# Stick-breaking attention: TensorE's work laid down in groups by a string, the mask as two 64-row products per head, one scan and one product for two heads

## The chip, the cores and the metric

The kernel runs on one core of a Trainium2 chip. The metric is the device time of the program in microseconds: 917.52 before, the median of three runs (916.94 to 918.17).

## What is computed

One decoder layer over 512 tokens of width 1024, in float32: a half-step SwiGLU feed-forward (FFN), then a mixer whose two halves, a gated linear recurrence (RG-LRU) and stick-breaking attention with 8 heads of 64, read one normalised input and end in one output projection, then a second FFN. The part that is changed is the attention:

```python
z = jnp.einsum("bhqd,bhkd->bhqk", qb, kf)
causal = k_pos[None, :] < q_pos[:, None]
log_beta = jax.nn.log_sigmoid(z)
log_1m = jnp.where(causal, jax.nn.log_sigmoid(-z), 0.0)
tail = lax.cumsum(log_1m, axis=log_1m.ndim - 1, reverse=True) - log_1m
w = jnp.where(causal, jnp.exp(log_beta + tail), 0.0)
return jnp.einsum("bhqk,bhkd->bhqd", w, vf)
```

A weight is thus sigmoid(z) at its key times the product of sigmoid(-z) over all later keys before the query. The kernel computes it in that form: two sigmoids, a running product from right to left, one multiplication.

## The kernel before

Matrix products run in float32r, a form that keeps part of the mantissa; each operand is split into a high and a low part (`h`, `l`), and three products (high-high, high-low, low-high) stand for one. `mm3` (line 135) issues the three. ScalarE makes the high part, VectorE the low one.

The program runs FFN a, the mixer and FFN b one after another. Within the mixer come the projections for the recurrence and for q, k and v; `turn("k", nk)` (called from line 757) transposes the normalised k by 128-row blocks into `ptk`, from which ScalarE writes `kTh` and VectorE `kTl` (lines 731, 732). It is called after step 27 of the 32 steps of the v projection; `rnn_out` (products `gel`, then `yrh` and `yrl`) is called after step 13. Then comes the attention stage.

There the queries of a head fall into blocks of 128. A unit is one pair of heads with query block 3 (512 keys), block 2 (384 keys), or blocks 1 and 0 (256 + 128), so there are 12 units in 4 pairs. A unit passes through these steps:

- `weigh` (line 799): the scores `pz`. Each head has 64 rows of q and k, so its product takes half of TensorE's rows; the two heads of a pair take one half each. Then the causal mask is added into PSUM by a bf16 product of 128 rows per head (line 821): the identity times `fut`, which holds -1e30 above the diagonal. ScalarE writes `s` = sigmoid(-z) and `be` = sigmoid(z) (lines 826, 828). VectorE runs one scan per head and query block (line 831), `rest`, and multiplies `be` by it (line 841).
- `turn_weights` (line 844): TensorE transposes `be` into `pw`, and ScalarE copies it to `wt` (line 859).
- `attend` (line 862), once for a pair: v times `wt` into `py`, the two heads in two halves of the columns (tiles of 128 rows by 64 columns).
- `take` splits `py` into `yah` and `yal` and sums squares for the attention norm.

Between them stands `project_out(k, 0, ...)` (line 768): the recurrence's part of one 128-row block of the output projection, 12 products `po`, which VectorE adds to x (line 781). Its weights are split as `h_o`, `l_o`. Behind the stage come the attention's part of the projection (24 products for each two blocks) and FFN b.

Each engine works through its own list in order. The order in the lists comes from a scheduler that simulates a timeline; `tc.issue_after` binds an instruction behind another. Which `weigh` and which `project_out` stand after which `turn_weights` is set by the numbers in WEIGH, FILL and REST. PSUM tiles come from pools (`psum("att", z=4, w=3, y=1)`): four banks in turn for `pz` and `po`, three for `pw`, one for `py`; a tile waits until the last reader of the bank's earlier tile is done.

Of the kernel before, what the change touches and what calls it, by code (L numbers as in the profile page):

```python
# [15 lines left out]
P = 128  # L16
T = 512
# [18 lines left out]

WEIGH = (1, 4, 5, 7, 9, 10, 13, 15, 16, 19)
FILL = (4, 8, 12, 16)
REST = (18, 23, 23)
# [9 lines left out]
def hybrid_layer_kernel(  # L49
# [61 lines left out]
    ident_b = const.tile([P, P], BF16, tag="ident_b", name="ident_b")  # L111
    nc.vector.tensor_copy(ident_b, ident)
    fut_b = const.tile([P, P], BF16, tag="fut_b", name="fut_b")
    nc.vector.tensor_copy(fut_b, fut)
# [20 lines left out]
    def mm3(out_, wh, wl, ah, al, start, stop):  # L135
        nc.tensor.matmul(out_, wh, ah, start=start, stop=False)  # L136
        nc.tensor.matmul(out_, wh, al, start=False, stop=False)  # L137
        nc.tensor.matmul(out_, wl, ah, start=False, stop=stop)  # L138
# [612 lines left out]
    def gate_and_recur():  # L751
# [6 lines left out]
        2, "v", {9: lambda: yn.rsqrt(DR, "b"), 13: rnn_out, 27: lambda: turn("k", nk)}  # L758
# [11 lines left out]
    def project_out(k, c, yh, yl, tag, ws, after=None):  # L770
        wh, wl = ws
        pt = bank(f"po{c}_{k}", tag)
        with tc.issue_after(after.ins) if after else nullcontext():
            for j in range(NJ):
                s = slice(j * P, (j + 1) * P)
                mm3(pt, wh[:, s], wl[:, s], yh[j], yl[j], j == 0, j == NJ - 1)
# [16 lines left out]
    with tc.tile_pool(name="att", bufs=2, reuse_waits="tile") as ap:  # L793
        beta = {}
        yah, yal = [], []
        na = Normed("t")

        def weigh(qbs, pair):
# [3 lines left out]
            parts = []  # L802
            for qb in qbs:
                n = (qb + 1) * P
                nn = max(n, 256)
                parts.append((col, n))
                both = None
                for a, b in (("qh", "kh"), ("qh", "kl"), ("ql", "kh")):
                    with tc.issue_after(both.ins) if both else nullcontext():
                        for pz, h in zip(pzs, pair):  # L810
                            j, rows = h // 2, slice((h % 2) * HD, (h % 2 + 1) * HD)
                            both = nc.tensor.matmul(
                                pz[:, col : col + nn],
                                qkT[a][rows, j, qb * P : (qb + 1) * P],
                                qkT[b][rows, j, :nn],
                                start=a + b == "qhkh",
                                stop=False,
                            )
# [4 lines left out]
            for pz, h in zip(pzs, pair):  # L823
                u = f"{qbs[0]}_{h}"
                s = ap.tile([P, T], F32, tag="s", name=f"s{u}")
                nc.scalar.activation(s[:, :col], pz[:, :col], AF.Sigmoid, scale=-1.0)
                be = ap.tile([P, T], F32, tag="be", name=f"be{u}", bufs=5)
                nc.scalar.activation(be[:, :col], pz[:, :col], AF.Sigmoid)
# [197 lines left out]
```

## Time and profile before

| What | Value |
|---|---|
| median of three runs | 917.52 us |
| profiled execution | 917.45 us, its span 915.7 us |
| TensorE busy (PE) | 909.1 us, 99% |
| VectorE busy (DVE) | 668.7 us, 73% |
| ScalarE busy (ACT) | 443.7 us, 48% |
| GpSimd busy (POOL) | 77.0 us, 8% |
| chain that ended last | PE 98%, DVE 1%, ACT 0% |

The span runs from the first to the last instruction of the profiled execution. An engine's share says in how much of it an instruction was under way; TensorE's instructions overlap, so a stretch can count as busy and still hold gaps in which no column is fed. The chain follows the work that ended last backwards. In the rows, L812 is line 812; PE is TensorE, DVE VectorE, ACT ScalarE, POOL GpSimd; a tile such as 64*128 is rows by columns of TensorE's array, and the PEclk of a window is the mean granted clock as a share of 2.4 GHz.

### The profile page before, as it was taken

The numbers are of one execution on the slowest core, as the hardware profiler recorded it, in microseconds if no ns is written. First come the engines' busy times: TensorE is split into PE (matmuls) and PEld (weight loads), VectorE is DVE, ScalarE is ACT, GpSimd is POOL, SyncE is SP. The second block draws the span as 40 slices with busy tenths as digits, with TensorE's granted clock in tenths as the row PEclk, the third lists the DMA queues.
The fourth block names the chain that finished last, engine by engine and source line by source line (L and its number), as shares of the span: only waits on it lengthen the run. The fifth ranks groups of instructions, "written<-read, shape, count | busy, mean of one in ns | idle before, by whom it ended". The sixth has DMA issues, their size and how long they took to land.

```text
span 915.7 us, 13632 instructions
## 1 busy us (share of the span) xinstructions
PE 909.1 (99%) x5410; PEld 798.7 (87%) x5410; DVE 668.7 (73%) x1031; ACT 443.7 (48%) x745; POOL 77.0 (8%) x57
## 2 busy tenths in 40 slices
PE   9999999999999999999999999999999999999998
PEld 8888899889988998888876678888899989998997
DVE  7599788658865859855689858399679756884663
ACT  7343456335533546445666744443356424642450
POOL 0000000000000005644030010500000000000000
PEclk9999999999999999999999999999999999999999
DMA  8532123502351123322111123522222422242102
GB/s 270 200 124 58 46 102 129 161 26 93 109 170 62 48 92 113 111 98 71 47 57 37 47 93 119 203 75 70 70 92 93 161 69 93 93 161 87 47 25 92
DMA packets 27807, 89.51 MB, mean 98 GB/s; under 512 B 3040, under 2 KB 6368, under 8 KB 23648
## 3 DMA queue, kind: packets, MB, share of 16 engines
q1 hardware_dynamic: 27744, 88.65, 28.7%
q8 instruction: 42, 0.69, 0.3%
q14 instruction: 21, 0.17, 0.1%
HBM read 86.54 MB, written 2.10 MB: 97 GB/s over the span
## 4 chain that ended last, share of the span: by engine, by line
PE 98%; DVE 1%; ACT 0%; issue 0%
PE pxgb L371 5%; PE pxga L371 5%; PE pxub L371 5%; PE pxua L371 5%; PE pdb L136 4%; PE pdb L138 4%; PE pdb L137 4%; PE pda L136 4%; PE pda L138 4%; PE pda L137 4%; PE pygb L371 4%; PE pyga L371 4%; PE pyua L371 4%; PE pyub L371 4%; PE first_p L501 4%; PE po L136 2%
## 5 line engine op out<-in xcount | busy, mean ns | idle before, releaser
L137 PE MATMUL pdb<-hlb,h_db 128*128 128x512 f32 (+1 forms) x180 | 68.7, 385 | 0.0
L138 PE MATMUL pdb<-hhb,l_db 128*128 128x512 f32 (+1 forms) x180 | 68.7, 385 | 0.0
L137 PE MATMUL pda<-hla,h_da 128*128 128x512 f32 x176 | 68.0, 389 | 0.0
L138 PE MATMUL pda<-hha,l_da 128*128 128x512 f32 x176 | 67.9, 389 | 0.0
L136 PE MATMUL pdb<-hhb,h_db 128*128 128x512 f32 (+1 forms) x180 | 67.3, 385 | 0.0
L136 PE MATMUL pda<-hha,h_da 128*128 128x512 f32 x176 | 66.2, 389 | 0.0
L441 DVE SCALAR_TENSOR_TENSOR x<-pdb,x 128x512 f32<-128x512 f32 (+1 forms) x33 | 21.9, 673 | 49.0 <-PE pdb L138 49.0
L441 DVE SCALAR_TENSOR_TENSOR x<-pda,x 128x512 f32<-128x512 f32 x32 | 21.8, 688 | 39.9 <-PE pda L138 39.9
L126 ACT CAST h_da<-r_da 128x768 fp32r<-128x768 f32 (+1 forms) x28 | 24.1, 868 | 48.2 <-PE pda L137 21.0
L126 ACT CAST h_db<-r_db 128x768 fp32r<-128x768 f32 (+1 forms) x28 | 24.3, 868 | 45.5 <-PE pdb L137 22.9
L137 PEld LDWEIGHTS pdb<-hlb,h_db 128*128 128x128 f32 x180 | 33.8, 188 | 6.6
L138 PEld LDWEIGHTS pdb<-hhb,l_db 128*128 128x128 f32 x180 | 33.8, 188 | 6.5
L136 PEld LDWEIGHTS pdb<-hhb,h_db 128*128 128x128 f32 x180 | 33.8, 188 | 6.5
L137 PEld LDWEIGHTS pda<-hla,h_da 128*128 128x128 f32 x176 | 33.1, 188 | 6.7
L138 PEld LDWEIGHTS pda<-hha,l_da 128*128 128x128 f32 x176 | 33.1, 188 | 6.7
L136 PEld LDWEIGHTS pda<-hha,h_da 128*128 128x128 f32 x176 | 33.1, 188 | 6.6
L166 POOL TENSOR_TENSOR sqa_m<-sqa_m,sq_m 128x512 f32<-128x512 f32 x7 | 11.8, 1690 | 313.3 <-ACT sq_m L165 313.1
L371 PE MATMUL pxga<-xh_sa,l_ga 128*128 128x256 f32 x128 | 36.2, 283 | 0.0
L371 PE MATMUL pxgb<-xh_sb,l_gb 128*128 128x256 f32 x128 | 36.2, 283 | 0.0
L371 PE MATMUL pxga<-xl_sa,h_ga 128*128 128x256 f32 x128 | 36.2, 283 | 0.0
L371 PE MATMUL pxgb<-xl_sb,h_gb 128*128 128x256 f32 x128 | 36.2, 283 | 0.0
L371 PE MATMUL pxua<-xh_sa,l_ua 128*128 128x256 f32 x128 | 36.2, 283 | 0.0
(397 smaller groups left out, 3105.3 us busy)
## 6 DMA issues: line engine op xcount, KB each, us to landing
r_da<-in_wd SPq DMA_DIRECT2D x24, 384.0 KB, 3.3
r_db<-in_wd SPq DMA_DIRECT2D x24, 384.0 KB, 3.2
rga<-in_wg SPq DMA_DIRECT2D x8, 1024.0 KB, 4.8
rua<-in_wu SPq DMA_DIRECT2D x8, 1024.0 KB, 4.7
rgb<-in_wg SPq DMA_DIRECT2D x8, 1024.0 KB, 5.5
rub<-in_wu SPq DMA_DIRECT2D x8, 1024.0 KB, 4.8
r_gb<-in_wg SPq DMA_DIRECT2D x6, 512.0 KB, 3.1
r_ub<-in_wu SPq DMA_DIRECT2D x6, 512.0 KB, 3.5
```

The costliest lines, as they stand in the source:

```text
L126: nc.scalar.copy(hi, raw)
L136: nc.tensor.matmul(out_, wh, ah, start=start, stop=False)
L137: nc.tensor.matmul(out_, wh, al, start=False, stop=False)
L138: nc.tensor.matmul(out_, wl, ah, start=False, stop=stop)
L166: (engine or nc.gpsimd).tensor_add(self.acc, self.acc, sq)
L371: nc.tensor.matmul(pt, l[:, s], r, start=start and k == 0 and i == 0, stop=k == KD // 2 - 1 and i == 2, skip_group_check=True,)
L441: nc.vector.scalar_tensor_tensor(x[k][:, t], pt[:, t], 0.5, x[k][:, t], op0=ALU.mult, op1=ALU.add)
L501: nc.tensor.matmul(pts[i], wp[i][:, s], xp[k], start=k == 0 and wp is hi and xp is n1.h, stop=k == KD - 1 and wp is lo,)
```

## The change

The three tables of numbers give way to one string, STEPS. Its letters stand for one `weigh` (Z), one `turn_weights` for a whole unit (W), one `project_out` of the recurrence's part (F) and one `attend` with `take` (P); every group of TensorE instructions is bound behind the last instruction of the group before it. The mask's identity and `fut` are stored as two halves of 64 rows, once for each half of the array, and each head adds its mask by two products of 64 rows on its own half. `s`, `be` and `rest` hold two heads side by side, and one scan and one product run over a unit. To start anew at each head and query block, the scan takes the maximum with `marks`, a tensor that is 1 at the starts and 0 elsewhere (the product stays at or below 1), in place of adding zero. `turn("k", ...)` comes after step 22 instead of 27. The buffers of `be` go from 5 to 3 (of twice the size), those of `rest` from 2 to 1.

```diff
-WEIGH = (1, 4, 5, 7, 9, 10, 13, 15, 16, 19)
-FILL = (4, 8, 12, 16)
-REST = (18, 23, 23)
+STEPS = "ZFZFZWZFWZWFZWZPWZFWZWZPWZFWZWPWWFPF"
...
+    halves_b = []
+    for src, n in ((ident, "ident_b"), (fut, "fut_b")):
+        t = const.tile([P, 2, P], BF16, tag=n, name=n)
+        for half in range(2):
+            for to in range(2):
+                nc.vector.tensor_copy(t[to * HD : (to + 1) * HD, half, :], src[half * HD : (half + 1) * HD, :])
...
-        2, "v", {9: lambda: yn.rsqrt(DR, "b"), 13: rnn_out, 27: lambda: turn("k", nk)}
+        2, "v", {9: lambda: yn.rsqrt(DR, "b"), 13: rnn_out, 22: lambda: turn("k", nk)}
...
+        def step():
+
+            return tc.issue_after(last[-1].ins) if last else nullcontext()
...
-                for pz in pzs:
-                    nc.tensor.matmul(pz[:, col + n - P : col + n], ident_b, fut_b, start=False, stop=True)
+                for half in range(2):
+                    with step():
+                        for i in range(2):
+                            rows = slice(i * HD, (i + 1) * HD)
+                            both = nc.tensor.matmul(
+                                pzs[i][:, col + n - P : col + n],
+                                ident_b[rows, half, :],
+                                fut_b[rows, half, :],
+                                start=False,
+                                stop=half == 1,
+                            )
+                    last.append(both)
...
-                for c, n in parts:
-                    nc.vector.tensor_tensor_scan(
-                        rest[:, c : c + n - 1][:, ::-1],
-                        s[:, c + 1 : c + n][:, ::-1],
-                        zero.to_broadcast([P, n - 1]),
-                        1.0,
-                        op0=ALU.mult,
-                        op1=ALU.add,
-                    )
-                for c, n in parts:
-                    w = be[:, c : c + n - 1]
-                    nc.vector.tensor_mul(w, w, rest[:, c : c + n - 1])
+            flat = [t.rearrange("p h c -> p (h c)") for t in (s, be, rest)]
+            n = 2 * col - 1
+            nc.vector.tensor_tensor_scan(
+                flat[2][:, :n][:, ::-1],
+                flat[0][:, 1:][:, ::-1],
+                marks[qbs][:, 1:][:, ::-1],
+                1.0,
+                op0=ALU.mult,
+                op1=ALU.max,
+            )
+            nc.vector.tensor_mul(flat[1][:, :n], flat[1][:, :n], flat[2][:, :n])
...
+        for what in STEPS:
+            if what == "Z":
+                scored.append(weigh(*units[len(scored)]))
+            elif what == "W":
...
+                turn_weights(qbs, scored[turned], ws[pair])
+                turned += 1
+            elif what == "F":
+                w = weights_out(done_f, 0, 1)
+                with step():
+                    project_out(done_f, 0, yrh, yrl, "z", *w)
+                last.append(project_out.last)
+                done_f += 1
+            else:
+                py = bank(f"py{done_p}", "y")
+                attend(pairs[done_p], py, ws[pairs[done_p]])
+                take(done_p, py)
+                done_p += 1
```

Three places in the lists show what moves. First VectorE between the sums of the recurrence's norm (`m_r`) and the first split that follows; `kTl` appears once for each block of 128 tokens. Before:

```order
L181 TENSOR_SCALAR m_r<-pst_r 128x4
L128 TENSOR_TENSOR l_o_2_4889<-r_o_2_4885,h_o_2_4887 128x512
L658 TENSOR_TENSOR gel_3770<-gel_3770,rb_r 128x512
L658 TENSOR_TENSOR gel_3790<-gel_3790,rb_r 128x512
L658 TENSOR_TENSOR gel_4058<-gel_4058,rb_r 128x512
L658 TENSOR_TENSOR gel_4181<-gel_4181,rb_r 128x512
L732 SCALAR_TENSOR_TENSOR kTl<-ptk_4548,vec,kTh 128x4x128
L732 SCALAR_TENSOR_TENSOR kTl<-ptk_4555,vec,kTh 128x4x128
L732 SCALAR_TENSOR_TENSOR kTl<-ptk_4562,vec,kTh 128x4x128
L662 SCALAR_TENSOR_TENSOR yrl_4477<-gel_3770,vec,yrh_4475 128x512
L662 SCALAR_TENSOR_TENSOR yrl_4482<-gel_3790,vec,yrh_4480 128x512
L732 SCALAR_TENSOR_TENSOR kTl<-ptk_4569,vec,kTh 128x4x128
```

Now, from the first `kTl` on:

```order
L734 SCALAR_TENSOR_TENSOR kTl<-ptk_4533,vec,kTh 128x4x128
L734 SCALAR_TENSOR_TENSOR kTl<-ptk_4540,vec,kTh 128x4x128
L734 SCALAR_TENSOR_TENSOR kTl<-ptk_4547,vec,kTh 128x4x128
L130 TENSOR_TENSOR l_o_2_4776<-r_o_2_4772,h_o_2_4774 128x512
L660 TENSOR_TENSOR gel_3776<-gel_3776,rb_r 128x512
L660 TENSOR_TENSOR gel_3796<-gel_3796,rb_r 128x512
L660 TENSOR_TENSOR gel_4064<-gel_4064,rb_r 128x512
L660 TENSOR_TENSOR gel_4187<-gel_4187,rb_r 128x512
L664 SCALAR_TENSOR_TENSOR yrl_4483<-gel_3776,vec,yrh_4481 128x512
L664 SCALAR_TENSOR_TENSOR yrl_4488<-gel_3796,vec,yrh_4486 128x512
L664 SCALAR_TENSOR_TENSOR yrl_4493<-gel_4064,vec,yrh_4491 128x512
L734 SCALAR_TENSOR_TENSOR kTl<-ptk_4554,vec,kTh 128x4x128
```

Three quarters of `kTl` stand ahead of the `gel` products now; the fourth stands behind them and behind three `yrl`.

Second, TensorE at the first `attend` (`py`; the names `wt_` are the two heads' weights). Before:

```order
L812 MATMUL pz_2_4844<-kTh,qTh 128x256
L812 MATMUL pz_3_4845<-kTh,qTh 128x256
L866 MATMUL py_4815<-wt_4675,v_4591 64x512
L849 MATMUL pw_3_4838<-ident,be_3_4760 128x128
L866 MATMUL py_4815<-wt_4676,v_4591 64x512
L866 MATMUL py_4815<-wt_4675,v_4593 64x384
L866 MATMUL py_4815<-wt_4676,v_4593 64x384
L866 MATMUL py_4815<-wt_4675,v_4595 64x256
L866 MATMUL py_4815<-wt_4676,v_4595 64x256
L866 MATMUL py_4815<-wt_4675,v_4597 64x128
L866 MATMUL py_4815<-wt_4676,v_4597 64x128
L849 MATMUL pw_3_4838<-ident,be_3_4760 128x128 x3
```

Now:

```order
L844 LDWEIGHTS ident_b
L844 MATMUL pz_5_4901<-fut_b,ident_b 128x128
L899 MATMUL py_4921<-wt_4737,v_4597 64x512
L899 MATMUL py_4921<-wt_4738,v_4597 64x512
L899 MATMUL py_4921<-wt_4737,v_4599 64x384
L899 MATMUL py_4921<-wt_4738,v_4599 64x384
L899 MATMUL py_4921<-wt_4737,v_4601 64x256
L899 MATMUL py_4921<-wt_4738,v_4601 64x256
L899 MATMUL py_4921<-wt_4737,v_4603 64x128
L899 MATMUL py_4921<-wt_4738,v_4603 64x128
L880 MATMUL pw_0_4936<-ident,be_2_4815 128x128 x3
L880 MATMUL pw_1_4937<-ident,be_2_4815 128x128 x3
```

Before, a transpose of the second head's weights stands inside the group, and the scores of the unit around it are cut too; now each group stands whole.

Third, VectorE from the first scan on. Before:

```order
L831 SCALAR_TENSOR_TENSOR rest_0_4621<-s_0_4617,zero 128x511
L841 TENSOR_TENSOR be_0_4619<-be_0_4619,rest_0_4621 128x511
L831 SCALAR_TENSOR_TENSOR rest_1_4628<-s_1_4624,zero 128x511
L841 TENSOR_TENSOR be_1_4626<-be_1_4626,rest_1_4628 128x511
L831 SCALAR_TENSOR_TENSOR rest_0_4645<-s_0_4641,zero 128x383
L831 SCALAR_TENSOR_TENSOR rest_1_4652<-s_1_4648,zero 128x383
L841 TENSOR_TENSOR be_0_4643<-be_0_4643,rest_0_4645 128x383
L841 TENSOR_TENSOR be_1_4650<-be_1_4650,rest_1_4652 128x383
L781 TENSOR_TENSOR x_91<-po_0_4661,x_91 128x512
```

Now:

```order
L863 SCALAR_TENSOR_TENSOR rest_0_4638<-s_0_4636,marks_4613 128x1023
L871 TENSOR_TENSOR be_0_4637<-be_0_4637,rest_0_4638 128x1023
L783 TENSOR_TENSOR x_97<-po_0_4651,x_97 128x512
L130 TENSOR_TENSOR l_o_4_4971<-r_o_4_4967,h_o_4_4969 128x512
L863 SCALAR_TENSOR_TENSOR rest_0_4679<-s_0_4677,marks_4616 128x767
L871 TENSOR_TENSOR be_0_4678<-be_0_4678,rest_0_4679 128x767
L783 TENSOR_TENSOR x_98<-po_1_4692,x_98 128x512
```

The scans (listed under the name of their instruction class) of two heads are one; the sum of the second output block into x, which frees a bank of `pz`, stands behind the second unit.

## Rows read from the trace of the kernel before

**Rows 1.** Windows of two stretches: time, busy us (instructions) per engine, PEclk, DMA.
```profile
474.00:484.00 10.00, 8.16 (x41) 5.34 (x40) 9.79 (x14) 7.91 (x16) 0.00 (x0) 0.83 0.08 28
474.70:544.70 70.00, 67.65 (x385) 45.60 (x385) 56.52 (x91) 46.53 (x101) 2.86 (x2) 0.98 0.15 53
```

**Rows 2.** TensorE timeline: start, us, engine, line, op, tiles, [idle <-releaser].
```profile
474.67 0.51 PE L812 MATMUL pz<-kTh,qTh 64*128 64x512 f32 x2
477.01 0.51 PE L812 MATMUL pz<-kTl,qTh 64*128 64x512 f32 x2 [1.84 <-DVE kTl L732]
```

**Rows 3.** Waits from 474 to 545: engine, releaser, total us, times, longest.
```profile
DVE rest L831 <- ACT s L826: 1.9, 3, 1.2
PE pw L849 <- DVE be L841: 0.5, 1, 0.5
```

**Rows 4.** VectorE timeline before the first scan.
```profile
470.50 2.50 DVE L658 TENSOR_TENSOR gel<-gel,rb_r 128x512 f32<-128x512 f32 x4 [2.08 <-ACT rb_r L197]
476.21 0.75 DVE L732 SCALAR_TENSOR_TENSOR kTl<-ptk,vec,kTh 128x512 fp32r<-128x512 f32 x1
```

**Rows 5.** TensorE timeline: transposes, score products, mask, transposes.
```profile
502.07 0.49 PE L849 MATMUL pw<-ident,be 128*128 128x128 f32 x3
502.49 0.50 PE L812 MATMUL pz<-kTh,qTh 64*128 64x512 f32 x2
502.83 0.40 PE L812 MATMUL pz<-kTl,qTh 64*128 64x512 f32 x2
503.07 0.39 PE L812 MATMUL pz<-kTh,qTl 64*128 64x512 f32 x2
503.39 0.29 PE L821 MATMUL pz<-fut_b,ident_b 128*128 128x128 bf16 x2
503.51 0.39 PE L849 MATMUL pw<-ident,be 128*128 128x128 f32 x2
```

**Rows 6.** TensorE timeline: attend in two pieces, and in one.
```profile
494.37 1.07 PE L866 MATMUL py<-wt,v 128*64 128x512 f32 x2
495.63 2.37 PE L866 MATMUL py<-wt,v 128*64 128x512 f32 x14
...
509.44 2.37 PE L866 MATMUL py<-wt,v 128*64 128x512 f32 x16
```

**Rows 7.** VectorE timeline: scans, products, sum into x, split.
```profile
504.33 1.22 DVE L831 TENSOR_TENSOR_SCAN rest<-s,zero 128x511 f32<-128x511 f32 x1 [0.56 <-ACT s L826]
505.66 0.69 DVE L841 TENSOR_TENSOR be<-be,rest 128x511 f32<-128x511 f32 x1
508.19 0.95 DVE L831 TENSOR_TENSOR_SCAN rest<-s,zero 128x383 f32<-128x383 f32 x1
509.28 0.56 DVE L841 TENSOR_TENSOR be<-be,rest 128x383 f32<-128x383 f32 x1
510.62 0.67 DVE L781 TENSOR_TENSOR x<-po,x 128x512 f32<-128x512 f32 x1
511.20 0.69 DVE L128 TENSOR_TENSOR l_o<-r_o,h_o 128x512 fp32r<-128x512 f32 x1
```

**Rows 8.** VectorE timeline: a scan over two tensors.
```profile
451.48 2.34 DVE L649 TENSOR_TENSOR_SCAN tau<-dec,ix 128x512 f32<-128x512 f32 x2
```

**Rows 9.** ScalarE timeline: sigmoids of the first score tile.
```profile
477.95 0.60 ACT L826 ACTIVATE s<-pz 128x512 f32<-128x512 f32 x1 [0.47 <-PE pz L821]
478.44 0.59 ACT L828 ACTIVATE be<-pz 128x512 f32<-128x512 f32 x1
```

**Rows 10.** VectorE timeline: the last products with the scans.
```profile
530.82 0.60 DVE L841 TENSOR_TENSOR be<-be,rest 128x255 f32<-128x255 f32 x2
```

**Rows 11.** TensorE timeline: after those products, and the FFN's first product.
```profile
531.71 0.47 PE L136 MATMUL po<-yah,h_o 128*128 128x512 f32 x1
...
564.52 0.39 PE L136 MATMUL pgb<-xh_b,h_gb 128*128 128x512 f32 x1
```

**Rows 12.** VectorE timeline: its first weights.
```profile
4.50 0.29 DVE L483 CAST first_h<-first_r 128x256 fp32r<-128x256 f32 x1 [2.69 <-DMA first_r<-in_wg]
```

More of the change, by code (lines that the diff above doesn't have):

```diff
@@ L793, in hybrid_layer_kernel @@
     with tc.tile_pool(name="att", bufs=2, reuse_waits="tile") as ap:
-        beta = {}
         yah, yal = [], []
         na = Normed("t")
+        marks = {}
+        for qbs in ((3,), (2,), (1, 0)):
+            w = sum(qb + 1 for qb in qbs) * P
+            m = ap.tile([P, 2 * w], F32, tag=f"m{qbs[0]}", name=f"marks{qbs[0]}", bufs=1)
+            nc.gpsimd.memset(m, 0.0)
+            for head in range(2):
+                c = head * w
+                for qb in qbs:
+                    c += (qb + 1) * P
+                    if c < 2 * w:
+                        nc.gpsimd.memset(m[:, c - 1 : c], 1.0)
+            marks[qbs] = m
+        last = []
+        def step():
+            return tc.issue_after(last[-1].ins) if last else nullcontext()
         def weigh(qbs, pair):
@@ new lines, in weigh @@
+                col += n
+            u = f"{qbs[0]}_{pair[0]}"
+            s = ap.tile([P, 2, col], F32, tag="s", name=f"s{u}")
+            be = ap.tile([P, 2, col], F32, tag="be", name=f"be{u}", bufs=3)
+            rest = ap.tile([P, 2, col], F32, tag="rest", name=f"rest{u}", bufs=1)
+            for i in range(2):
+                nc.scalar.activation(s[:, i, :], pzs[i][:, :col], AF.Sigmoid, scale=-1.0)
+            for i in range(2):
+                nc.scalar.activation(be[:, i, :], pzs[i][:, :col], AF.Sigmoid)
@@ new lines, in weigh, with turn_weights @@
+            flat = [t.rearrange("p h c -> p (h c)") for t in (s, be, rest)]
[9 more added lines that the diff above has]
+            nc.vector.tensor_mul(flat[1][:, :n], flat[1][:, :n], flat[2][:, :n])
+            return be
+        def turn_weights(qbs, be, ws):
+            nb = sum(qb + 1 for qb in qbs)
+            pws = [bank(f"pw{qbs[0]}_{i}", "w") for i in range(2)]
+            for i, (pw, wt) in enumerate(zip(pws, ws)):
+                with step():
+                    for b in range(nb):
+                        turned = nc.tensor.transpose(
+                            pw[:, b * P : (b + 1) * P], be[:, i, b * P : (b + 1) * P], ident
+                        )
+                last.append(turned)
+                c = 0
+                for qb in qbs:
+                    n = qb + 1
+                    src = pw[:, c * P : (c + n) * P].rearrange("p (b q) -> p b q", b=n)
+                    first = max(qb - 2, 0) * P
+                    q = slice(qb * P - first, (qb + 1) * P - first)
+                    to = wt[:, first : first + 4 * W].rearrange("p (b q) -> p b q", b=4)[:, :n, q]
+                    nc.scalar.copy(to, src)
+                    c += n
@@ L862, in attend @@
         def attend(pair, py, ws):
             for b in range(NB):
[L865 to L872 removed]
+                with step():
+                    for i, h in enumerate(pair):
+                        both = nc.tensor.matmul(
+                            py[i * HD : (i + 1) * HD, b * P :],
+                            v[b][:, h * HD : (h + 1) * HD],
+                            ws[i][:, b * W + b * P : b * W + T],
+                            start=b == 0,
+                            stop=b == NB - 1,
+                        )
@@ L874, in take @@
+                last.append(both)
         def take(j, py):
```

94 lines of the change are left out of this document (16 added, 78 removed).

## The prediction

> **What bounds the kernel now.** I read the busy time by stage first, then TensorE's timeline across the attention stage, then who waits for whom there, then VectorE's timeline. In the 70 us from the first score product on, TensorE has work in 67.65 us, VectorE in 56.52 and ScalarE in 46.53 [rows 1]: TensorE ends the stage, VectorE stands close behind it. In those records TensorE truly waits only twice, 1.84 us for the last quarter of kTl [rows 2] and 0.5 us for weights that VectorE had not multiplied yet [rows 3]. The rest of its loss lies inside its busy time: the half clock after the first wait, the gaps when it changes between tiles of 64 and 128 rows, and attend products that run alone. So the question is how much of that the new order takes away, and whether VectorE can follow.
>
> **TensorE, term by term.** The wait for kTl. VectorE stands idle 2.08 us before the four gel products [rows 4] and makes all of kTl behind them; the last quarter starts at 476.21 and takes 0.75, so pz resumes at 477.01 [rows 2, 4]. In the new order three quarters of kTl come ahead of gel, in that idle time. The fourth comes behind four gel products and three yrl, which are of its own kind: 470.50 + 2.44 + 3 x 0.67 + 0.75 = 475.7 (each starts 0.08 before the last one ends), or about 475.2 if the copy of rb_r comes half a microsecond sooner because nothing stands before it on TensorE. pz asks for it one pair after 474.67, at 475.0. So 0.2 to 0.7 of the 1.84 us stay; I take 0.3, a gain of 1.5.
>
> The clock. From 474 to 484 the granted clock averages 0.83 [rows 1], that is, some of it ran at 1.2 instead of 2.4 GHz, right after the wait of 1.84 us; 0.17 of 10 us is 1.7 us of work lost. With the wait at 0.3 I count it as gained.
>
> Changes of tile. Three transposes 0.11 apart from 502.07 on should let pz start at 502.40; it starts at 502.49 (+0.09). The first pair of pz products takes 0.34 to the next, the second 0.24 (+0.10), the third, before the mask product of 128 rows, 0.32 (+0.08) [rows 5]. A trip into the 64-row tiles and back costs 0.27. Counted over the two orders, from the first pz to the sums of the attention norm, the tile shape changes 58 times before and 29 times now (the mask keeps the shape, and the groups are no longer cut): 14.5 trips, 3.9 us. The mask itself: 64 products of 64 rows stand for 32 of 128. The old ones took 0.06 each (two from 503.39 to 503.51) [rows 5]. If the two heads' halves run beside each other, as the pz pairs do (both in 0.51 [rows 2]), they take the time of 32; if not, 32 x 0.06 = 1.9 us more, which VectorE's pace, below, would partly cover. I take the first, because it is the same pair of tiles.
>
> Attend. In the order before, one of the two heads' first products stands apart in three of the four pairs: that lone one takes 1.07, and the remaining 14 rows still 2.37, as long as a whole group of 16 elsewhere [rows 6]. A loss of 1.0 each, of which 0.2 are tile changes counted already: 3 x 0.8 = 2.4.
>
> Sum for TensorE alone: 1.5 + 1.7 + 3.9 + 2.4 = 9.5 us.
>
> **VectorE, which must keep up.** Scans: 511 columns 1.22, 383 columns 0.95 [rows 7], so 0.0021 us per column and 0.14 fixed. The new scan reads a real tensor of marks and takes a maximum, where the old one read a broadcast zero and added. The trace has a scan over two real tensors: 512 columns twice in 2.34, at most 1.17 each [rows 8], so I price marks at nothing; the maximum is not in the trace, see the last rival. 1023 columns then take 2.28, 767 take 1.74. The product waits 0.11 for its scan (504.33 + 1.22 to 505.66) and takes 0.69 for 511 and 0.56 for 383 [rows 7], hence 1.22 and 0.95, of which 0.08 overlap the next. One unit: 2.28 + 0.11 + 1.22 - 0.08 = 3.53, or 1.74 + 0.11 + 0.95 - 0.08 = 2.72. All twelve: 4 x 3.53 + 8 x 2.72 = 35.9. Between the first scan and the last product of the new order stand six sums into x, four splits of 512 columns and two yal, at 0.58 to 0.67 [rows 7], and two splits of 1024: 12 x 0.6 + 2 x 1.15 = 9.5. Together 45.4 us without a pause.
>
> The first scan now needs both heads: the mask is done at 475.9, two s and one be come 0.49 apart and the last takes 0.60 [rows 9], so it starts at 475.9 + 0.15 + 0.98 + 0.60 = 477.6. The last product ends at 477.6 + 45.4 + 0.1 = 523.1; before, at 530.82 + 0.60 = 531.4 [rows 10]. From there TensorE before still had the work from 531.71 to the next FFN at 564.52 [rows 11], 32.8 us. Now, behind the last product, it has six transposes (0.7 with their wait) and the same output products, with the attend whole: 0.7 + 32.8 - 1.0 = 32.5. End: 523.1 + 32.5 = 555.6, 8.9 us sooner. That is less than TensorE's 9.5: **VectorE sets the pace now.**
>
> What stops TensorE instead. pz and po share four PSUM banks in turn; the second head of unit 4 gets the bank of po_1, which is free when VectorE has added po_1 to x, behind the product of unit 2. VectorE: 477.6 + 3.53 + 0.58 + 0.6 + 2.72 + 0.67 = 485.7. TensorE is there at 475.9 + 2.9 (po_0) + 0.9 + 2.9 + 1.2 + 0.9 = 484.7. So it waits about 1 us, and likewise, shorter, at units 7 and 10. These waits lie within the 8.9, but the clock may fall after them. I deduct 0.7 for that (two fifths of 1.7) and 0.8 for VectorE waiting for s, which it does for 1.9 us in all before [rows 3]. Forecast: 8.9 - 1.5 = 7.4 gained.
>
> **What costs nothing.** Eight copies of 64 rows instead of two at the start: they run before VectorE's first weights, for which it waits 2.69 us [rows 12]. The fills of the marks are on GpSimd, which does nothing from 474 to 484 [rows 1], and the unit that asks for the last of them is the third. ScalarE does the same activations of the same size.
>
> **Rivals.** (a) TensorE's gain arrives whole: VectorE's 0.8 of waits is not there and the clock stays up, while the kTl wait goes entirely. 9.5 + 0.3 = 9.8 gained, 907.7. For it: VectorE already waits for s in only three places. Against: it has no slack left in the new order.
>
> (b) The clock falls after each of the three new waits. The one case in the trace is a wait of 1.84 us, after which the mean clock is 0.83 [rows 1, 2]; after 0.5 us nothing falls. At 1 us it may go either way. Three times 1.7 us, little of it covered: 8.9 - 5.1 = 3.8 gained, 913.7. The Trainium skill has this in "TensorE: Matmul & The Clock Gate", section "A second HAM failure mode: psum-queue depth-cycling": cycling through PSUM banks can leave so many short idle spots between groups of products that the clock swings between its two levels. By that rule the time would be the one just given; the case before shows it once.
>
> (c) The change does not do what it says: TensorE's gaps in that stage are covered by what it waits for anyway, and the regrouping only moves them. Then the wait and its clock are all that goes, 1.5 + 1.7 = 3.2 gained, 914.3. Against it: TensorE's records show no waits there to cover them [rows 3].
>
> (d) Slower: a scan with a maximum against marks read backwards. It decides over 4 x 1023 + 8 x 767 = 10,228 columns, and VectorE has no slack, so each 0.001 us per column is 10.2 us. From 0.0009 more (0.0021 to 0.0030) the gain is gone; half as much again, 0.00105, gives 10.7 - 8.9 = 1.8 lost, 919.3. For it: no row shows a maximum. Against: the scan with other tensors costs the same [rows 8].
>
> **How the numbers follow.** The profiled execution took 917.45 us, 0.07 under the median of the three runs. Forecast 917.45 - 7.4 = 910.0, chance 0.62; its own range is 908.5 to 912. Rivals: (a) 0.13, (b) 0.11, (c) 0.08, (d) 0.06. The range of 907.2 to 914.0 holds the forecast, (a) and (b) and leaves out most of (c) and (d). About 0.2% either way, 1.8 us, is what a measurement here can tell from no change: faster 0.90, within it 0.04, slower 0.06.
>
> **What would show it.** Right: pz<-kTl waits under 0.7 us and the clock stays at full around 477; VectorE goes from the first scan to the last product with under 2 us of pauses, 46 to 47 us; TensorE waits for x at units 4, 7 and 10; attend is four blocks of 2.37; a scan of 1023 columns takes 2.3. Wrong: a scan above 3 us, mask products in the 64-row tiles apart by more than 0.12, or a granted clock under 0.9 in several stretches.

## The result, and the profile after

912.21 us (median of 4 runs, 910.77 to 912.53) against 917.62 before (4 runs, 916.94 to 918.17): a ratio of 0.9938, interval 0.9921 to 0.9956. That is 5.4 us faster; the forecast was 7.4. The profiled execution took 912.53 us, its span 910.8.

| | before | after |
|---|---|---|
| profiled execution, span | 917.45, 915.7 | 912.53, 910.8 |
| first score product | 474.67 | 475.75 |
| first scan on VectorE | 478.80 | 478.82 |
| end of the last product with the scans | 531.4 | 526.0 |
| first product of FFN b | 564.52 | 559.60 |

From the first product of FFN b to the end both take 351.2 us (915.7 - 564.52 and 910.8 - 559.60), so all of the difference lies in the attention stage. There VectorE starts its first scan at the same time in both kernels and ends its last product with the scans 5.4 us sooner; what TensorE has left behind that is 0.5 longer (33.1 to 33.6). Of VectorE's 52.6 us before, 4.4 were idle: three waits for `s` [rows 3] and three for the high part of the attention's output, which in the view of VectorE's waits from 474 to 530 is this row:

```profile
DVE yal L879 <- ACT yah L877: 2.5, 3, 1.4
```

In the changed kernel none of that idle time is left. First the windows after, which answer to [rows 1]:

```profile
474.00:484.00 10.00, 10.00 (x60) 7.16 (x60) 8.30 (x10) 8.06 (x16) 0.00 (x0) 1.00 0.09 28
475.80:545.80 70.00, 66.89 (x448) 49.41 (x448) 53.39 (x49) 45.38 (x100) 6.54 (x4) 0.98 0.18 63
524.00:534.00 10.00, 7.83 (x31) 6.15 (x33) 4.47 (x5) 3.03 (x8) 1.28 (x1) 0.83 0.15 54
```

At 474 the clock is now at full; the fall that [rows 1] show there stands at 524 instead. TensorE's timeline says what lies around it, the answer to [rows 2, 5 and 11]:

```profile
467.41 0.63 PE L728 MATMUL ptk<-ident,natk 128*128 128x128 f32 x4 [0.62 <-DVE m_r L183]
475.75 0.50 PE L830 MATMUL pz<-kTh,qTh 64*128 64x512 f32 x2
476.09 0.39 PE L830 MATMUL pz<-kTl,qTh 64*128 64x512 f32 x2
487.02 0.49 PE L830 MATMUL pz<-kTh,qTh 64*128 64x512 f32 x1 [0.76 <-DVE x L783]
510.78 2.37 PE L899 MATMUL py<-wt,v 128*64 128x512 f32 x16
526.17 1.51 PE L880 MATMUL pw<-ident,be 128*128 128x128 f32 x6 [2.35 <-DVE be L871]
527.33 0.78 PE L138 MATMUL po<-yrh,h_o 128*128 128x512 f32 x1
559.60 0.39 PE L138 MATMUL pgb<-xh_b,h_gb 128*128 128x512 f32 x1
```

The wait for kTl is gone and each attend is one block of 2.37. In their place stand three waits: 0.62 for a block of the normalised k (the row names m_r, which VectorE finished just then; the transposes read natk), 0.76 for x at unit 4, and 2.35 for VectorE's last product. Behind that one TensorE runs at 1.2 GHz, until about 529.5 (the first po takes 0.78 instead of 0.50).

VectorE from the first scan on, the answer to [rows 7 and 10]:

```profile
478.82 2.29 DVE L863 TENSOR_TENSOR_SCAN rest<-s,marks 128x1023 f32<-128x1023 f32 x1 [1.43 <-ACT s L858]
481.21 1.23 DVE L871 TENSOR_TENSOR be<-be,rest 128x1023 f32<-128x1023 f32 x1
482.35 0.68 DVE L783 TENSOR_TENSOR x<-po,x 128x512 f32<-128x512 f32 x1
...
487.48 1.75 DVE L863 TENSOR_TENSOR_SCAN rest<-s,marks 128x767 f32<-128x767 f32 x1
489.33 0.96 DVE L871 TENSOR_TENSOR be<-be,rest 128x767 f32<-128x767 f32 x1
490.39 2.29 DVE L863 TENSOR_TENSOR_SCAN rest<-s,marks 128x1023 f32<-128x1023 f32 x1
...
519.78 1.75 DVE L871 TENSOR_TENSOR be<-be,rest 128x767 f32<-128x767 f32 x1
...
525.06 0.96 DVE L871 TENSOR_TENSOR be<-be,rest 128x767 f32<-128x767 f32 x1
```

No row between the first scan and the last product has an idle time: VectorE is the pace, for 47.2 us. A scan with marks and a maximum costs what the old one did per column (2.29 for 1023). Two things are slower than they need be. Where a scan follows a product with nothing between, it starts 1.06 behind the product's start; where something stands between, that starts 0.88 behind (485.40 to 486.28): the one buffer of `rest` is still being read. And the product at 519.78 takes 1.75 instead of 0.96, beside this row of GpSimd:

```profile
518.70 2.01 POOL L168 TENSOR_TENSOR sqa_t<-sqa_t,sq_t 128x512 f32<-128x512 f32 x1 [47.80 <-ACT sq_t L167]
```

The product starts in the middle of it and ends 0.82 behind its end, about its own length. The addition itself begins under the scan of 517.91, which keeps its 1.74, and takes 2.01 where the next one takes 1.28 (at 528.26). The Trainium skill ("SBUF — State Buffer", section "Who interferes with whom") says that a VectorE instruction with two inputs in SBUF and a GpSimd instruction that reads SBUF exclude each other; these rows agree.

ScalarE ahead of the first scan, the answer to [rows 9]:

```profile
476.56 0.70 ACT L765 ACTIVATE v<-pv,r_m 128x512 f32<-128x512 f32 x1
477.14 0.61 ACT L858 ACTIVATE s<-pz 128x512 f32<-128x512 f32 x1
477.61 0.62 ACT L860 ACTIVATE be<-pz 128x512 f32<-128x512 f32 x1
478.09 0.63 ACT L858 ACTIVATE s<-pz 128x512 f32<-128x512 f32 x1
```

The scan needs both `s`; between them stands a `be`, and ahead of them the last copy of v.

### The profile page after: what moved, and what is told of

Its sections match the earlier page's. It is cut to its first block, busy times and chain, and to the rows that moved or that the text cites. A ratio compares the mean times of both kernels' runs of the same rounds, so it can differ in the third digit from the quotient of the medians.

```text
span 910.8 us, 13645 instructions
## 1 busy us (share of the span) xinstructions
PE 902.8 (99%) x5442; PEld 797.8 (88%) x5442; DVE 668.1 (73%) x997; ACT 442.9 (49%) x745; POOL 80.5 (9%) x65
## 4 chain that ended last, share of the span: by engine, by line
PE 94%; DVE 3%; ACT 1%; issue 1%; POOL 1%; DVEq 0%; POOLq 0%
PE pxga L373 5%; PE pxgb L373 5%; PE pxub L373 5%; PE pxua L373 5%; PE pdb L140 4%; PE pdb L139 4%; PE pdb L138 4%; PE pda L138 4%; PE pda L139 4%; PE pda L140 4%; PE pygb L373 4%; PE pyga L373 4%; PE pyub L373 4%; PE pyua L373 4%; PE first_p L503 4%; PE po L138 2%
## 5 line engine op out<-in xcount | busy, mean ns | idle before, releaser
L128 ACT CAST h_db<-r_db 128x768 fp32r<-128x768 f32 (+1 forms) x28 | 24.3, 868 | 45.5 <-PE pdb L139 22.8
L140 PEld LDWEIGHTS pda<-hha,l_da 128*128 128x128 f32 x176 | 33.1, 188 | 6.7
L138 PEld LDWEIGHTS pda<-hha,h_da 128*128 128x128 f32 x176 | 33.1, 188 | 6.7
L139 PEld LDWEIGHTS pda<-hla,h_da 128*128 128x128 f32 x176 | 33.1, 188 | 6.7
```

The lines of the kernel that those rows point to most:

```text
L128: nc.scalar.copy(hi, raw)
L140: return nc.tensor.matmul(out_, wl, ah, start=False, stop=stop)
```

## The experiments

Each ratio is to the kernel before, run on the same chip.

| run | us | ratio, interval |
|---|---|---|
| changed kernel | 912.21 | 0.9938, 0.9921 to 0.9956 |
| e1, before with k turned at 22 | 916.45 | 0.9984, 0.9976 to 0.9993 |
| e2, changed with k turned at 27 | 913.11 | 0.9948, 0.9934 to 0.9961 |
| e3, changed with the mask of 128 rows | 910.86 | 0.9931, 0.9918 to 0.9943 |
| e4, changed with a fill before the last transposes | 908.23 | 0.9896, 0.9883 to 0.9910 |
| e5, changed with a scan per head | 911.53 | 0.9932, 0.9918 to 0.9946 |
| e8, before with merged scans | 915.37 | 0.9973, 0.9964 to 0.9983 |
| e9, changed without products | 906.59 | 0.9879, 0.9866 to 0.9893 |
| e10, e4 with the first fills in pw's banks | 908.37 | 0.9898, 0.9885 to 0.9912 |
| e11, e10 with k turned at 23 | 907.64 | 0.9894, 0.9878 to 0.9911 |
| e12, e11 with the scan in place | 907.54 | 0.9891, 0.9877 to 0.9906 |
| e13, e12 with both s first | 906.59 | 0.9882, 0.9867 to 0.9897 |
| e14, e4 with a scan per head | 909.79 | 0.9915, 0.9901 to 0.9928 |

The second table is worked out from TensorE's timelines: for each product the time from its start to the start of the next, summed over the tile that it writes, from the first score product to the first product of FFN b; in brackets the waits among it.

| | first pz | first pgb | pz | pw | py | po |
|---|---|---|---|---|---|---|
| before | 474.67 | 564.52 | 19.39 (2.32) | 10.53 | 12.21 | 46.45 |
| e1 | 475.75 | 563.50 | 18.04 (1.56) | 10.64 | 12.21 | 45.59 |
| e8 | 474.67 | 562.23 | 21.05 (4.25) | 9.92 | 10.21 | 45.22 |
| after | 475.75 | 559.60 | 14.18 (0.76) | 13.01 (2.35) | 9.22 | 46.27 |
| e2 | 475.26 | 559.59 | 14.64 (1.84) | 12.47 (2.36) | 9.22 | 46.84 |
| e3 | 475.76 | 559.66 | 14.79 (0.70) | 12.03 (2.23) | 9.22 | 46.70 |
| e4 | 475.25 | 555.01 | 14.15 (0.76) | 9.81 | 9.22 | 45.42 |
| e9 | 475.58 | 553.65 | 12.34 | 10.11 | 9.22 | 45.24 |
| e13 | 474.34 | 553.40 | 13.51 (0.37) | 9.78 | 9.22 | 45.39 |

**What TensorE's order is worth by itself (e9).**

```diff
-            nc.vector.tensor_mul(flat[1][:, :n], flat[1][:, :n], flat[2][:, :n])
```

> The changed kernel without the 12 products of be and rest (the weights are the plain sigmoids): VectorE has 12.5 us less to do and TensorE waits for ScalarE alone. It measures what TensorE's order is worth by itself. By the forecast's sum for TensorE (9.5 us less than before): 908.1, with the granted clock at full and no wait before the last transposes. If TensorE's terms were too large, as the 1.1 us later start of the scores suggests (0.62 of a new wait and extra gaps): 908.5 to 910. If VectorE does not set the pace: 912.2.

Without its 12 products this kernel computes plain sigmoids as weights; it serves only to time TensorE's order. Measured 906.59, 11.1 us under the kernel before, with no wait left in the stage. So the order gives TensorE more than the sum of 9.5, not less, and VectorE's pace, with the half clock behind its last wait, keeps 5.6 us of it (912.21 - 906.59) back.

**The wait at the end (e4).**

```diff
-STEPS = "ZFZFZWZFWZWFZWZPWZFWZWZPWZFWZWPWWFPF"
+STEPS = "ZFZFZWZFWZWFZWZPWZFWZWZPWZFWZWPWFWPF"
```

> The changed kernel, with the one block of the recurrence's output products (2.9 us) that stands behind the last transposes put ahead of them (STEPS ends in WFWPF, not WWFPF). Theory: VectorE's last product at 526.0 sets the end, TensorE idles 2.35 us for it and then runs 3.4 us at half clock. The block fills that wait, so the wait and the half clock (1.7) both go and 0.4 stays, since TensorE comes to the transposes at 526.6: 3.7 gained, 908.5. If the half clock comes anyway, from the short wait at unit 4 or elsewhere: 2.0 gained, 910.2. If TensorE then waits for the copies of the last weights instead, which the block hides now: 1 to 2 gained, 910.5 to 911. If VectorE does not set the end: 912.2.

Measured 908.23, 4.0 under the changed kernel; 3.7 was expected. TensorE's timeline of this run at the last transposes:

```profile
522.43 0.88 PE L880 MATMUL pw<-ident,be 128*128 128x128 f32 x6
523.06 0.48 PE L138 MATMUL po<-yrh,h_o 128*128 128x512 f32 x1
...
525.89 0.82 PE L880 MATMUL pw<-ident,be 128*128 128x128 f32 x6
526.46 0.48 PE L138 MATMUL po<-yah,h_o 128*128 128x512 f32 x1
```

The block fills the time in which TensorE stood idle; there is no wait and no product at half speed behind it. About 1.5 of the 4.0 is that half clock: the one execution of the changed kernel whose mean granted clock is 1.000 took 910.77. One letter moved in a string gives nearly as much as the whole change.

**The transposes of k (e1, e2, e11).** Three numbers in one place:

```diff
-        2, "v", {9: ..., 13: rnn_out, 27: lambda: turn("k", nk)}
+        2, "v", {9: ..., 13: rnn_out, 22: lambda: turn("k", nk)}
```

e1 does this to the kernel before, e2 undoes it in the changed one, e11 has 23 (on e10, below).

> The kernel before, with the transposes of k called after step 22 instead of 27 and nothing else. By the forecast's two first terms the wait for kTl (1.5) and the half clock behind it (1.7) go, less what the trace after shows as new, a wait of 0.62 for natk and about 0.4 of extra gaps around the cut groups of transposes: 2.2 gained, 915.4. If TensorE's gaps of that stage are covered by something else: within 0.5 of 917.6. If this alone makes the whole change: 912 to 913.

> The changed kernel with the transposes of k called after step 27 again. VectorE's list is then that of before up to the first scan (the gel products ahead of kTl), so the wait for kTl of about 1.8 us and the half clock behind it return, and the mask is done 1 us later than in the changed kernel. If VectorE's chain sets the end: its first scan starts up to 1 us later and TensorE's lost clock is covered by the wait that it has at the end anyway, 912.5 to 913.2. If TensorE sets the end: 0.9 of wait and 1.7 of clock come on top, 914.8.

> The kernel of the run before (fill ahead of the last transposes, first two fills in the banks of pw; 908.4) with the transposes of k after step 23 in place of 22. The trace after shows TensorE 0.62 us idle there for the third block of natk; one step (0.7 us) later it should find it done, so that scores and first scan come 0.6 sooner and the end with them: 907.8. If the last quarter of kTl is then asked for too early: a wait of 0.4 at the second score pair and 908.2 to 908.4.

e1 gains 1.2 us, not 2.2. The second pair of scores starts at 476.09 instead of 477.01 and the clock stays up, but TensorE now catches up with VectorE:

```profile
PE pw L849 <- DVE be L841: 1.1, 2, 0.6
PE ptk L726 <- DVE m_r L181: 0.6, 1, 0.6
PE pw L849 <- DVE x L781: 0.5, 1, 0.5
```

Before, only 0.5 of these stood in the stage [rows 3]. What arrives is what VectorE gains: its first scan starts 0.9 sooner (477.87) and its last product with the scans ends 1.0 sooner (530.39). The half clock cost the kernel before next to nothing. Among its executions run beside these experiments, the 13 with a mean granted clock of 1.000, in which no such fall can lie, took 917.5 in the median, and the 29 with 0.997 or 0.998 took 917.7 (two with 0.996 took 919.0 and 919.25). So TensorE made the lost 1.7 up; by e1's rows, where it would otherwise have waited for VectorE.

e2 loses 0.9 in the median (the intervals overlap), which fits VectorE setting the end and not TensorE (2.6). Its waits and two of its windows:

```profile
PE pw L880 <- DVE be L871: 2.4, 1, 2.4
PE pz L830 <- DVE kTl L734: 1.8, 1, 1.8
```

```profile
474.00:484.00 10.00, 8.16 (x39) 5.47 (x38) 9.20 (x12) 6.88 (x13) 0.00 (x0) 0.83 0.10 28
524.00:534.00 10.00, 7.64 (x45) 5.68 (x43) 6.00 (x6) 4.44 (x10) 1.29 (x1) 1.00 0.15 54
```

Here the clock falls behind the wait of 1.8 and not behind that of 2.4; in the changed kernel's profile it fell behind the wait of 2.35. VectorE's last product ends 1.5 later than there (527.56), but no half clock lies behind it, and the first product of FFN b comes at the same time within 0.02 us. e11 takes the wait of 0.62 away and gains 0.7 on e10 (0.5 when each is taken against the kernel before on its own chip); 0.6 was expected.

**The mask (e3).** One product of 128 rows per head and block in place of two of 64, with the two constants stored as whole tiles again:

```diff
-                for half in range(2):
-                    with step():
-                        for i in range(2):
-                            rows = slice(i * HD, (i + 1) * HD)
-                            both = nc.tensor.matmul(..., ident_b[rows, half, :], fut_b[rows, half, :], ...)
-                    last.append(both)
+                with step():
+                    for pz in pzs:
+                        both = nc.tensor.matmul(pz[:, col + n - P : col + n], ident_b, fut_b, start=False, stop=True)
+                last.append(both)
```

> The changed kernel with the mask of before, one product of 128 rows per head and query block; the groups stay. Tile shapes change 39 times from the first score product to the sums of the attention norm, in place of 29; at 0.09 each that is 0.9 us of TensorE's time. If VectorE's chain sets the end, the wait before the last transposes shrinks by that and the time stays at 912.2 within 0.4. If TensorE sets it: 913.1. If a tile change costs more than the 0.09 that rows of before show, as the gain of the run without products suggests (5.0 in place of 3.9 us for 29 changes): 0.13 each, and TensorE's score slots 1.3 us longer.

Measured 910.86 (five runs: 910.5 to 910.9 three times, 912.5 and 912.6), where the changed kernel has 910.77 once and 912.1 to 912.5 three times: the same two levels, the lower with a mean granted clock of 0.999 or 1.000, the upper with 0.997 or 0.998. In the second table pz is 0.61 longer, pw and po together 0.55 shorter, most of it a change of shape that moved from behind the mask to ahead of it (at the first unit the slot ahead of the mask takes 0.33 instead of 0.24, the mask's own 0.10 instead of 0.21). All slots without their waits: 80.74 in the changed kernel, 80.97 here. The mask by itself is worth about 0.2 us of TensorE's time and nothing that can be measured of the kernel's.

**The merged scan (e8, e5, e14).** e8 puts it into the kernel before; e5 takes it out of the changed kernel, e14 out of e4:

```diff
-            n = 2 * col - 1
-            nc.vector.tensor_tensor_scan(
...
-            nc.vector.tensor_mul(flat[1][:, :n], flat[1][:, :n], flat[2][:, :n])
+            for i in range(2):
+                c = 0
+                for qb in qbs:
+                    n = (qb + 1) * P
+                    nc.vector.tensor_tensor_scan(
+                        rest[:, i, c : c + n - 1][:, ::-1],
+                        s[:, i, c + 1 : c + n][:, ::-1],
+                        zero.to_broadcast([P, n - 1]),
...
+                c = 0
+                for qb in qbs:
+                    n = (qb + 1) * P
+                    w = be[:, i, c : c + n - 1]
+                    nc.vector.tensor_mul(w, w, rest[:, i, c : c + n - 1])
+                    c += n
```

> The kernel before with the scans and products of two heads made one (marks, maximum) and nothing else. If merging relieves VectorE by its 20 fewer scans and products: 1 us or more faster, 916.5. If it is worth nothing on VectorE, as the run with one scan per head in the changed order suggests (911.5 against 912.2), and only ties the first head's transposes to the second head's scan: 0 to 1.5 us slower than before, 918 to 919.

> The changed kernel with the scans and products of before: one per head and query block, 32 of each in place of 12, adding zero; the order and the masks stay. If VectorE sets the pace: 20 more of each at about 0.14 and 0.08 fixed is 4.4 us, less 1.3 for gaps between a scan and its own product that are filled again, less up to 1 because the first scan needs one head only: 2 us slower than the changed kernel, 914.2, and the wait before the last transposes grows by as much. If TensorE sets the pace: no difference, 912.2.

> The changed kernel with the fill ahead of the last transposes (908.2, clock at full throughout) and the scans and products of before, one per head and query block. It asks what the merged scan is worth where no fall of the clock blurs it. By the rows of the run with one scan per head, VectorE needs 9.10 us for the three units of a pair that way and 9.17 merged, and its first scan starts 1.3 us sooner: 0 to 0.8 faster than 908.2. If the gain of the kernel before with merged scans alone (2.3 us) came from the merging and not from its clock and whole attends: 1 to 2 us slower, 909.2 to 910.2.

e8 gains 2.3 us, e5 is 0.7 faster than the changed kernel's median (but 0.8 slower than its one execution at a mean clock of 1.000, and no execution of e5 is below 0.999), and e14 is 1.6 slower than e4. By their times e8 and e14 fit the branch that the merge relieves VectorE; e5 lies below both of its branches. The traces show that none of the three is the price of the merge alone. In e8 the wait for kTl is as long as before, and nothing falls behind it in the profile:

```profile
477.01 0.50 PE L825 MATMUL pz<-kTl,qTh 64*128 64x512 f32 x2 [1.84 <-DVE kTl L732]
```

```profile
474.00:484.00 10.00, 7.78 (x49) 5.11 (x48) 9.03 (x11) 7.69 (x16) 0.00 (x0) 1.00 0.09 28
```

The clock is not e8's gain, though: three executions of it with a mean clock of 1.000 took 915.16 to 915.57, six with 0.998 took 915.13 to 916.27. What its trace shows is VectorE: its first scan starts 0.8 later than before, and its last product ends at 529.53 instead of 531.42 [rows 10].

```profile
528.57 0.96 DVE L857 TENSOR_TENSOR be<-be,rest 128x767 f32<-128x767 f32 x1
```

All scans and products, each from its start to the next start and without idle time, take 36.95 there and 39.21 in the kernel before. In the kernel before, scan and product stand in turn for the most part, and the first unit of 512 keys takes 3.86 up to the next scan (3.53 merged, in the changed kernel):

```profile
478.80 1.22 DVE L831 TENSOR_TENSOR_SCAN rest<-s,zero 128x511 f32<-128x511 f32 x1
480.12 0.69 DVE L841 TENSOR_TENSOR be<-be,rest 128x511 f32<-128x511 f32 x1
480.73 1.21 DVE L831 TENSOR_TENSOR_SCAN rest<-s,zero 128x511 f32<-128x511 f32 x1
482.05 0.69 DVE L841 TENSOR_TENSOR be<-be,rest 128x511 f32<-128x511 f32 x1
482.66 1.80 DVE L831 TENSOR_TENSOR_SCAN rest<-s,zero 128x383 f32<-128x383 f32 x2
```

About 0.5 of those 2.3 us is a scan beside GpSimd. The order of TensorE's work changed with the merge as well (attend in fewer pieces, py 10.21 against 12.21; more waits, pz 4.25 against 2.32), and no run separates the two. In e14, whose scans and products stand two in a row, VectorE's own work is the same as merged, 37.54 against 37.62 in e4:

```profile
489.72 2.34 DVE L866 TENSOR_TENSOR_SCAN rest<-s,zero 128x511 f32<-128x511 f32 x2
491.97 1.27 DVE L879 TENSOR_TENSOR be<-be,rest 128x511 f32<-128x511 f32 x2
493.15 0.68 DVE L783 TENSOR_TENSOR x<-po,x 128x512 f32<-128x512 f32 x1
...
506.44 1.80 DVE L866 TENSOR_TENSOR_SCAN rest<-s,zero 128x383 f32<-128x383 f32 x2 [1.05 <-ACT s L858]
```

3.43 from scan to sum here, 3.53 merged. But it idles 1.05 us at two units for `s`, because ScalarE's list has another order there: the square of py, which waits for VectorE, stands ahead of the sigmoids.

```profile
505.43 0.60 ACT L164 ACTIVATE sqa_t<-py 128x512 f32<-128x512 f32 x1 [2.82 <-DVE yal L922]
505.93 0.86 ACT L858 ACTIVATE s<-pz 128x384 f32<-128x384 f32 x2
```

In e4 those sigmoids stand ahead of the square. So the scheduler's new order on ScalarE costs 2.1 us of VectorE's time, and the earlier first scan (2.03 behind the first score product instead of 3.06) gives 1.0 back. By these rows the merge saves VectorE about 1.7 us against scan and product in turn and close to nothing against two scans in a row; no run isolates it with ScalarE's order held.

**Taking VectorE's losses away (e10, e12, e13).** On e4, one edit on top of the other; e12 and e13 also hold e11's step 23:

```diff
-                    project_out(done_f, 0, yrh, yrl, "z", *w)
+                    project_out(done_f, 0, yrh, yrl, "w" if done_f < 2 else "z", *w)
```

```diff
-                flat[2][:, :n][:, ::-1],
+                flat[0][:, 1:][:, ::-1],
                 flat[0][:, 1:][:, ::-1],
...
-            nc.vector.tensor_mul(flat[1][:, :n], flat[1][:, :n], flat[2][:, :n])
+            nc.vector.tensor_mul(flat[1][:, :n], flat[1][:, :n], flat[0][:, 1:])
```

```diff
-                nc.scalar.activation(s[:, i, :], pzs[i][:, :col], AF.Sigmoid, scale=-1.0)
-            for i in range(2):
-                nc.scalar.activation(be[:, i, :], pzs[i][:, :col], AF.Sigmoid)
+                both = nc.scalar.activation(s[:, i, :], pzs[i][:, :col], AF.Sigmoid, scale=-1.0)
+            with tc.issue_after(both.ins):
+                for i in range(2):
+                    nc.scalar.activation(be[:, i, :], pzs[i][:, :col], AF.Sigmoid)
```

> The changed kernel with the fill ahead of the last transposes (908.2 in the run before) and, besides, the first two blocks of the output products in the banks of pw instead of those of pz. No score product then asks for a bank that an output block holds until VectorE has added it to x, up to unit 4. If the wait of 0.76 us at unit 4 and the score pairs out of step behind it (0.4 to 0.5) cost time: 0.8 to 1.2 gained on 908.2, 907.0 to 907.4; the floor is the run without products, 906.6. If VectorE's chain sets the end there too: 908.2, with the wait moved to the last transposes.

> The run with step 23, and the scan written over s, with three buffers of s in place of two of s and one of rest. In the trace after, a scan that follows a product directly starts 1.06 behind the product's start in place of 0.88, at three units, since the one buffer of rest is still being read. If that is so and VectorE sets the pace: those become 0.88 and the time falls by 0.5 against the run with step 23, to 907.3. If VectorE does not set the pace there: no difference.

> The run with the scan in place, and both s of a unit ahead of both be on ScalarE. The first scan, which in the trace after waits 1.43 us for the second s behind the first be, starts about 0.5 sooner. If VectorE sets the pace: 0.5 faster than the run with the scan in place, 906.8, with the waits of TensorE for x and the score pairs out of step shorter by as much. If the last transposes are then bound by TensorE itself: 0 to 0.3. The floor is the run without products, 906.6, less the 0.6 of the earlier scores.

e10 gains nothing: the wait for x is gone at unit 4 and stands at unit 7, 1.1 us long. A bank is not what is short; VectorE is late. e12 makes the scan start 0.88 behind the product, as expected, but only 0.1 of the 0.5 arrives in the median:

```profile
488.71 0.96 DVE L870 TENSOR_TENSOR be<-be,s 128x767 f32<-128x767 f32 x1
489.59 2.28 DVE L862 TENSOR_TENSOR_SCAN s<-s,marks 128x1023 f32<-128x1023 f32 x1
```

In its profile the stage is 0.4 shorter than in e11 (79.55 against 79.95 from first pz to first pgb) and starts 0.4 later. Nearly all of that is there before either kernel does anything new (the products of ones with `sqa_r`, ahead of the transposes of k, start at 463.15 against 462.78); over all profiles here that row lies anywhere from 462.5 to 463.6, so starts that differ by some tenths say nothing about an edit. e13 has its first scan 2.77 behind the first score product in place of 3.26, and gains 1.0:

```profile
477.11 2.29 DVE L863 TENSOR_TENSOR_SCAN s<-s,marks 128x1023 f32<-128x1023 f32 x1 [0.94 <-ACT s L857]
```

906.59 is the fastest kernel here that computes the whole, 10.9 us under the kernel before and 5.6 under the changed one; TensorE's wait for x is down to 0.4.

## Why the prediction was right, and where it was too high

The direction, the range (907.2 to 914.0) and the mechanism of the new kernel, VectorE's chain as its pace, held. The gain was put 2 us too high, and the time lies 0.2 outside the likeliest case's own range of 908.5 to 912. By the number alone 912.21 is nearer to rival (b)'s 913.7 than to 910.0; what speaks for the forecast is the trace, not the number.

**"VectorE sets the pace now"**: right; e4 and e13 gain by what they do to VectorE's chain and to what stands behind it. The step gave the end as first scan + VectorE's work + tail. Against 559.60 for the first product of FFN b it had 555.6, or 557.1 with the two deductions; the three parts were off by 4.0 together.

- First scan: 477.6 predicted, 478.82 measured, 1.2 late. I left the first scores at 474.67 and the second pair at 475.0, and didn't ask whether TensorE finds its transposes' operand ready when they are called five steps sooner. It doesn't: the scores come 1.08 later, by 0.62 of wait and one more cut in the v projection; 0.25 of it stands ahead of the transposes already. That step, "the last quarter of kTl", looked only at who consumes the moved work. Then ScalarE still had a copy of v to do.
- VectorE's work: 45.5 predicted, 47.2 measured, 1.7 more. Scans, products, sums and splits had their durations right. Left out were three scans that wait for a product's buffer (0.18 each, 0.5 in all) and the stretch beside GpSimd (0.8); the remaining 0.4 is in gaps of 0.13 instead of 0.11 and in yal.
- Tail: 32.5 predicted, 33.6 measured, 1.1 more: the half clock behind the last wait, 1.7, less 0.6 that is shorter elsewhere.

4.0 less the 1.5 deducted in advance is 2.5, and 557.1 + 2.5 = 559.6. That the deductions covered so much is partly luck: the 0.8 was for waits for `s`, of which there are none behind the first scan, and the 0.7 for a clock that falls after the waits for x, where it stayed up.

**TensorE's sum of 9.5**: too low; e9 shows 11.1. The kTl term of 1.5 was too high: the wait of 1.84 went, and the scores start 1.08 later. The clock's 1.7 is lost time of TensorE in the profile before, and e9 and e1 don't have it; but the kernel before takes as long in executions without such a fall, so as a gain of the kernel it was worth about 0.2. The same record speaks against the prediction's opening, that TensorE ends the stage of the kernel before: at least where the clock fell, its lost time was covered by VectorE's pace. Changes of tile, 3.9, were mis-sized and misnamed: from e1 to e9 pz falls by 4.1 without the waits (16.48 to 12.34), pw by 0.5 and po by 0.35, 5.0 together, but the mask's share is 0.2 by e3. A change of shape as such was priced too high: by e3 ten more of them cost 0.23 us, where 0.9 would follow. That groups and pairs stay whole is what is left to pay for the rest; it is argued, and no run has it alone. Attend, 2.4 and 0.6 among the tile changes: 12.21 - 9.22 = 3.0, as predicted.

**"What stops TensorE instead"**: half right. The wait for x came at unit 4 (0.76 of the 1.0), at units 7 and 10 it shows only as pairs of scores out of step. The rest of VectorE's lag collected at the end, 2.35 us, where the prediction named no wait of TensorE.

**The rivals.** (a) is what e9 measures and needs VectorE out of the way. (b), a clock that falls after each new wait, happened once and not three times, not behind a wait for a bank, and not always: see below. So the rule of the Trainium skill that it named, of a clock that swings between groups of products, no run here shows; the waits of 0.4 to 1.2 leave it at full in every profile, and the fall in the kernel before, which the prediction counted for it, stands behind a wait for kTl, not for a PSUM bank. (c) put the wait and its clock at 914.3 and the rest at nothing; e1, which does that alone, took 916.45, and e9 shows the rest. Its ground, that TensorE's losses are covered by what it waits for anyway, holds for the half clock of the kernel before. (d), the maximum, costs nothing: 2.29 for 1023 columns, 2.28 predicted.

## What to carry to other kernels

When an engine's list is made shorter, look where it will stand still next and put work there that needs nothing: the largest single gain here was a block moved in front of a wait that the change itself had made. For work that is moved forward, check both ends, who needs it and whether its operands are there. Before a half clock is counted as a gain, compare executions with and without it: here it cost one kernel about 1.5 us and another nothing. And before a stage is called balanced, add up what the other engine's buffers, ScalarE's order and GpSimd's neighbours cost it, since a scheduler that re-orders one engine can cost more than the edit saves.

## What the hardware showed that was not expected

- The fall of the clock is not decided by the length of the wait. Behind the wait of 1.84 us for kTl it fell in the profiles of the kernel before and of e2 and not in e8's, where the product behind it starts at 477.01 as before; behind 2.35 it fell in the changed kernel's profile and behind 2.2 in e3's, not behind 2.4 in e2's.
- The same loss of 1.7 us of TensorE's work costs one kernel nearly all of it and another nothing. Behind VectorE's last product nothing covers it: of four runs of the changed kernel the one whose mean granted clock is 1.000 took 910.77, the three others with 0.997 or 0.998 took 912.13 to 912.53. The kernel before and e8 take the same time with and without a fall.
- A product of VectorE on two SBUF operands took about 1.75 instead of 0.96 beside a GpSimd addition, in the profiles of the changed kernel, e2 to e4 and e10 to e13 alike. Before, the same addition fell on a scan, 1.69 for two where the next two took 0.99.
- A scan may be written over its own input in reverse order: 2.28 for 1023 columns, as with a buffer of its own.
